# Paired transposes, deferred normalisation and early factors in a two-layer hybrid encoder kernel

## The chip, the cores and the metric

The kernel runs on one core of a Trainium2 chip. The metric is device time in microseconds (us) of one execution; where several executions are given, it is their median. The profile of the kernel before comes from one further execution, taken by the hardware profiler.

## The reference

Two layers (DEPTH = 2) work on x of 512 positions by 2048. In each layer:

```python
h = rmsnorm(x, pre_norm_g[l])
z = h @ w_in[l]                                   # 2048 -> 4928 columns
q_lat, kv_lat, k_pe, gb, gc, xin, q_mem, gate = split_cols(z)
q  = rmsnorm(q_lat, q_norm_g[l]) @ w_uq[l]        # 512 -> 8 heads of 192
kv = rmsnorm(kv_lat, kv_norm_g[l]) @ w_ukv[l]     # 256 -> 8 heads of 256
# rotary positions on the last 64 of each q head and on k_pe, shared by all heads
a_out = mla_attention(q, k, v)                    # softmax over all 512 positions
c_out = gb * conv3(gc * xin)
m_out = memory_attention(q_mem, rmsnorm(mem), w_mk[l], w_mv[l])   # 4 heads, 256 tokens
y = concat(a_out, c_out, m_out) * silu(gate)
x = x + rmsnorm(y @ w_o[l], post_norm_g[l])
```

Everything is float32. The kernel keeps that precision by splitting each operand of a product into a high and a low part and adding three products.

## The kernel before

**Products.** Every float32 operand is split: ScalarE casts it to the high part (`wh`, line 177; line 257 for activations), VectorE subtracts that from the source and leaves the low part (`wl`, line 178; line 258). `mm3` (lines 250 to 254) then issues three matmuls per pair of operands: high by high (252), high by low (253), low by high (254). Which of the two operands comes first decides whether line 253 or line 254 is the one that needs the low part of the weights. The large projections (input and output) multiply blocks by a scheme with seven products in place of eight; its passes are called P1 to P7, and each step of a pass (`step`, line 524) holds twelve matmuls of 512 columns: one unit of weights of 128 x 1024 against two blocks of rows. Sums of weights are made by accumulating DMAs that GpSimd issues (line 154).

**Layer.** A layer runs through five groups of columns of the input projection (`gs[0]` to `gs[4]`; group 3 makes the latents q_lat, kv_lat and k_pe, group 4 makes half of the gate), the turning of latents and gates, in layer 0 the memory's keys and values, then `mixer`: sixteen query blocks of memory attention (four heads of four blocks of 128 queries), thirty-two of the main attention (eight heads), and the output projection `out_proj`, whose last part adds the residual and, in layer 0, makes the normalised rows that layer 1 starts from. The memory's keys and values of layer 1 are woven between the first transposes of layer 1.

**Order.** The instructions of TensorE, SyncE and GpSimd run in the order in which the program issues them. The order on VectorE and ScalarE is chosen when the program is compiled, among what is ready by the compiler's own estimate, earlier issued work first. On the chip each engine keeps to its order.

**Planner.** `Program.run` (lines 118 to 205) goes through a list of steps. Ahead of each step it loads and prepares (casts and subtracts) the weights of the step itself and of the two units behind it. After the step it adds the step's `room` to a balance (at most 2.5), and takes put-off work from a queue as long as the balance covers the cost of the queue's head. `pr.defer(cost, fn)` puts work in that queue; `pr.until(cond)` issues from it until a condition holds. A step of the passes has a room of 1.4, less where its end brings work for VectorE.

**Latents.** `latents_begin` (line 820), put between the fourth and the fifth step of group 4, squares the eight latent blocks on ScalarE (line 808), makes the factors on GpSimd (`rsqrt_mean`, lines 262 and 264, and line 811), and issues eight products on VectorE at once (line 813). From the seventeenth step of group 4 on, `latent_turn` transposes the normalised latents.

**Attention.** `head_iters` makes three parts of each query block: `score` (matmuls of the scores, maximum on VectorE, line 995; exponential on ScalarE, 998; reciprocal on VectorE, 1000; scaling on ScalarE, 1001), `trans` (transposes of the 128 x 512 or 128 x 256 weights on TensorE, line 1012, into a PSUM bank, then the split into `PT`), and `av` (the product with the values, for two query blocks together). `pipeline` (line 1050) strings them: in iteration k comes the score of block k, then other work given in `between` (projections of the next heads, rotary steps, turned rotary queries), then `trans` of block k-3, and in each second iteration `av` of the blocks up to k-5. All tiles in PSUM share eight banks.

**Residual.** When a block of 128 rows of the output projection has its four column quarters (`scale`, line 1147), `residual` (line 1189) puts four or five pieces of work in the queue: `factor` (sum of squares and the factor on GpSimd, cost 0.2), two halves of the residual product (`part`, line 1205 on VectorE, cost 1.2 each, each followed by a store that GpSimd issues), and in layer 0 `norm`, which squares all 2048 columns on ScalarE (line 573), makes the next layer's factor on GpSimd and scales all columns (line 579).

Of the kernel before, what the change touches and what calls it, by code (L numbers as in the profile page):

```python
# [8 lines left out]
AF = mybir.ActivationFunctionType  # L9
ALU = mybir.AluOpType  # L10
# [3 lines left out]
D = 2048  # L14
S = 512
KT = D // P
NT = S // P
# [7 lines left out]
EPS = 1e-6  # L25
# [55 lines left out]
class Program:  # L81
# [19 lines left out]
    def add(self, fn, units=(), room=0.0, ahead=None):  # L101

        self.steps.append((list(units), fn, room, self.ahead if ahead is None else ahead))
# [104 lines left out]
def encoder(tc, x, mem, positions, pre_norm_g, w_in, q_norm_g, w_uq, kv_norm_g, w_ukv, conv_w,  # L208
# [3 lines left out]
    nc = tc.nc  # L212
# [15 lines left out]
    pr = Program(nc, raw_p, hi_p, lo_p)  # L228
    add = pr.add

    G = {}
    n_id = [0]

    def nm(s):
        n_id[0] += 1
        return f"{s}_{n_id[0]}"
# [4 lines left out]
    def slab(name, dt=F32):  # L241
        return slabs.tile([P, D], dt, tag="slab", name=nm(name))

    def scrap(name, w=512, dt=F32):
        return piece.tile([P, 512], dt, tag="piece", name=nm(name))[:, :w]

    def small(w=1, tag="st"):
        return stat.tile([P, w], F32, tag=tag, name=nm(tag))
# [7 lines left out]
    def split_to(hi, lo, src):  # L256
        nc.scalar.copy(hi, src)  # L257
        nc.vector.tensor_tensor(lo, src, hi.bitcast(F32), op=ALU.subtract)  # L258

    def rsqrt_mean(ssq, n, w=1, more=EPS):  # L260
        ms = small(w, "ms")
        nc.gpsimd.tensor_scalar(ms, ssq, 1.0 / n, more, op0=ALU.mult, op1=ALU.add)
        r = small(w, "r")
        nc.gpsimd.tensor_tensor(r, ms, G["mhalf"][:, :w], op=ALU.pow)
        return r
# [305 lines left out]
    def row_factor(xt, junk):  # L571
        ssq = small()
        nc.scalar.activation(junk, xt, AF.Square, accum_out=ssq)
        return rsqrt_mean(ssq, D)

    def normalise_rows(xt, dst, on=None):
        r = row_factor(xt, dst)
        if on is nc.scalar:
            nc.scalar.activation(dst, xt, AF.Copy, scale=r)
        else:  # L580
            nc.vector.tensor_scalar_mul(dst, xt, r)
# [182 lines left out]
    def turn4(view, j, dst=None):  # L764

        ps = bank("tps")
        for t in range(NT):
            nc.tensor.transpose(ps[:, t * P:(t + 1) * P], view(t)[:, j * P:(j + 1) * P], G["ident"])  # L768
        return ps
# [6 lines left out]
    def gate_turn(j, view, c):  # L776
        def f():
            ps = turn4(view, c)
            nc.scalar.activation(y_slab(j // 4)[:, j % 4, :], ps, AF.Silu)
        return f  # L780
# [13 lines left out]
    def qm_turn(j, C):  # L794
        def f():
            if j == 0:
                G["Qm"] = tuple(slab(n, F32R).rearrange("p (i c) -> p i c", i=4) for n in ("QmH", "QmL"))
            ps = turn4(lambda t: C["qm"][:, t, :], j)
            hi, lo = G["Qm"][0][:, j, :], G["Qm"][1][:, j, :]
            nc.scalar.activation(hi, ps, AF.Copy, scale=SC_MEM)  # L800
            nc.vector.scalar_tensor_tensor(lo, ps, SC_MEM, hi.bitcast(F32), op0=ALU.mult, op1=ALU.subtract)
        return f

    def normalise(views, n, gain, by=None):
        junk, grow = scrap("junk", n), gain
        ssq = small(NT, "ssq4")
        for t, v in enumerate(views):
            nc.scalar.activation(junk, v, AF.Square, accum_out=ssq[:, t:t + 1])
        r = rsqrt_mean(ssq, n, NT)
        if by:  # L810
            nc.gpsimd.tensor_scalar(r, r, by, None, op0=ALU.mult)
        for t, v in enumerate(views):
            nc.vector.scalar_tensor_tensor(v, v, r[:, t:t + 1], grow, op0=ALU.mult, op1=ALU.mult)

    def latents_rows(l):
        G["grow"] = scrap("growq"), scrap("growk", KVR)
# [3 lines left out]
    def latents_begin(l, C):  # L820
        G["q"] = [v[:, :QR_] for v in C["lat"]]
        G["kv"] = [v[:, O_KV:O_KV + KVR] for v in C["lat"]]
        normalise(G["q"], QR_, G["grow"][0], SC_MLA)
        normalise(G["kv"], KVR, G["grow"][1])

    def k_rope(C):
        m = scrap("kpm").rearrange("p (b t s i) -> p b t s i", b=2, t=NT, s=2)
        m1, m2 = m[:, 0], m[:, 1]
        for t in range(NT):
            kp = C["lat"][t][:, O_PE:O_PE + ROPE].rearrange("p (s i) -> p s i", s=2)  # L830
            nc.vector.tensor_tensor(m1[:, t], kp, G["cos2"][:, t], op=ALU.mult)
            for s in range(2):
                nc.vector.tensor_tensor(m2[:, t, s, :], kp[:, 1 - s, :], G["sin2"][:, t, s, :], op=ALU.mult)
        nc.vector.tensor_tensor(m1, m1, m2, op=ALU.add)
        kr = m1.rearrange("p t s i -> p t (s i)")
        krA = scrap("krA", dt=F32R).rearrange("p (t d i) -> p t d i", t=NT, d=2)
        krB = scrap("krB", dt=F32R).rearrange("p (t d i) -> p t d i", t=NT, d=2)
        for d in range(2):
            nc.scalar.copy(krA[:, :, d, :], kr)
            nc.vector.tensor_tensor(krB[:, :, d, :], kr, krA[:, :, d, :].bitcast(F32), op=ALU.subtract)  # L840
        G["kr"] = krA, krB
# [7 lines left out]
            nc.scalar.copy(kab[:, n * S:(n + 1) * S], ps.bitcast(F32))  # L849
        G["KA"], G["KB"] = kab[:, :S], kab[:, S:2 * S]  # L850

    def latent_turn(tag, j):
        def f():
            if j == 0:
                if tag == "cq":
                    G["cq"] = tuple(slab(n, F32R).rearrange("p (k c) -> p k c", c=S) for n in ("cqH", "cqL"))
                else:
                    both = slab("ckv", F32R).rearrange("p (s k c) -> p s k c", s=2, k=2)
                    G["ckv"] = both[:, 0], both[:, 1]
            views = G["q" if tag == "cq" else "kv"]  # L860
            ps = turn4(lambda t: views[t], j)
            H, L = G[tag]
            split_to(H[:, j, :], L[:, j, :], ps)
        return f
# [184 lines left out]

    def pipeline(its, between):  # L1050

        n = len(its)
        for k in range(max(n + 6, max(between) + 1)):
            if k < n:
                add(*its[k][0])
            for s in between.get(k, ()):
                add(*s)
            if 0 <= k - 3 < n:
                add(its[k - 3][1])
            if 0 <= k - 5 < n and its[k - 5][2]:  # L1060
                add(its[k - 5][2])

# [7 lines left out]
    def mixer(l, C, gates, pair2, tail):  # L1070
# [27 lines left out]
        for pair in range(4):  # L1098
# [5 lines left out]
            for k, v in nxt.items():  # L1104
                between[m + 8 * pair + k] = v
        pipeline(its, between)


# [80 lines left out]
    def residual(l, st, t):  # L1189
        last = l == depth - 1  # L1190
        rows = slice(t * P, (t + 1) * P)
        og = st["og"][t]

        def factor():
            if last and t == NT - 1:
                st["r", t] = rsqrt_mean(st["ssq"][t][:, 2:3], D, more=st["pre"])
                return
            tot = small(1, "tot2")
            nc.vector.tensor_reduce(tot, st["ssq"][t], axis=AX.X, op=ALU.add)
            st["r", t] = rsqrt_mean(tot, D)  # L1200

        def part(c, n=1024):
            cs = slice(c, c + n)
            xt = st["x"][t]
            nc.vector.scalar_tensor_tensor(xt[:, cs], og[:, cs], st["r", t], xt[:, cs], op0=ALU.mult, op1=ALU.add)
            if last:
                nc.sync.dma_start(out[0][rows, cs], xt[:, cs])
            else:
                nc.gpsimd.dma_start(G["dst"][rows, cs], xt[:, cs])

        def norm():
            normalise_rows(st["x"].pop(t), og, on=nc.scalar)
            G[f"hs{t}"] = og

        pr.defer(0.2, factor)
        pr.defer(1.2, lambda: part(0))
        if last and t == NT - 1:
            pr.defer(0.7, lambda: part(1536, 512))
            pr.defer(0.7, lambda: part(1024, 512))
        else:  # L1220
            pr.defer(1.2, lambda: part(1024))
        if not last:
            pr.defer(0.0, norm)
# [8 lines left out]
    def put(*passes):  # L1232
        for steps in passes:
            for s in steps:
                add(*s)
# [26 lines left out]
    for l in range(depth):  # L1262
# [22 lines left out]
        else:  # L1285
# [3 lines left out]
            for n in range(16):  # L1289
                t, q = n // 4, n % 4  # L1290
# [41 lines left out]
        if l == 0:  # L1332
            add(positions_load)
        g4 = [s for steps in gs[4] for s in steps]
        put(g4[:4])
        add(lambda l=l, C=C: latents_begin(l, C))
        put(g4[4:8])
        if l > 0:
            add(lambda C=C: k_rope(C))
        put(g4[8:16])  # L1340
        if l == 0:
            add(mem_load)
            G["mTd"] = dram.tile([4, P, D], F32, name="mTd")
        lat = [latent_turn("cq", j) for j in range(4)] + [latent_turn("ckv", j) for j in range(2)] + [k_rope_turn] * (l > 0)
        gm = lambda t, C=C: C["gm"][:, t, :]
        more = [(f, []) for f in lat + [qm_turn(j, C) for j in range(4)] + [gate_turn(12 + j, gm, j) for j in range(4)]]
        if l == 0:
# [74 lines left out]
```

## Time and profile before

| | us |
|---|---|
| median of 3 runs (1511.77 to 1512.84) | 1511.78 |
| the profiled execution | 1512.46 |
| its span | 1510.7 |
| TensorE busy | 1488.4 |
| VectorE busy | 1054.7 |
| ScalarE busy | 869.3 |
| GpSimd busy | 291.3 |

The span is the time from the first to the last instruction of the profiled execution. In the rows of the timeline below the columns are: start from the span's beginning in us, duration in us, engine (PE is TensorE, ACT ScalarE, DVE VectorE, POOL GpSimd), line of the kernel, operation, output and inputs, shape, number of instructions merged in the row, and in brackets the engine's idle time before it with what ended the wait. Matmuls overlap: the duration of one of 512 columns is given as 0.39, but the next one starts 0.23 later, so time lost is read from the starts.

### The profile page before, as it was taken

How to read it: one execution, taken by the hardware profiler on the slowest of the kernel's cores; microseconds unless marked ns; L12 is line 12 of the kernel's file. 1: busy time of each engine (PE TensorE's matmuls, PEld its weight loads, DVE VectorE, ACT ScalarE, POOL GpSimd, SP SyncE). 2: the span in 40 equal slices, each digit the busy share in tenths (PEclk: the TensorE clock that was granted, in tenths of full speed). 3: DMA queues.
4: the chain of work that ended last, by engine and by line, in shares of the span. 5: the costliest groups of instructions: out<-in, count | busy, mean ns of one | idle time of the engine just before them, and what ended most of it. 6: DMA issues, size and time to landing. Idle time of an engine off the chain costs nothing.

```text
span 1510.7 us, 20218 instructions
## 1 busy us (share of the span) xinstructions
PE 1488.4 (99%) x7613; PEld 1277.4 (85%) x7613; DVE 1054.7 (70%) x1404; ACT 869.3 (58%) x1347; POOL 291.3 (19%) x289
## 2 busy tenths in 40 slices
PE   9999999999999999999999999999999999999997
PEld 7888888988898888888888888888988888888886
DVE  6965675555868668769788765675565486698687
ACT  7743534454767768645588533534454587686443
POOL 1233131332000000230220233121333000003212
PEclk9999999999999999999999999999999999999999
DMA  8999897989582111595987999897989521027945
GB/s 332 217 212 224 202 177 167 199 202 248 167 262 80 52 41 58 103 212 159 306 293 246 238 219 224 198 171 167 204 196 212 159 71 43 29 84 138 259 118 182
DMA packets 142580, 267.18 MB, mean 177 GB/s; under 512 B 17084, under 2 KB 39956, under 8 KB 139156
## 3 DMA queue, kind: packets, MB, share of 16 engines
q0 software_dynamic: 59072, 128.99, 44.3%
q1 hardware_dynamic: 83280, 136.88, 27.9%
q8 instruction: 59, 0.97, 0.3%
q14 instruction: 37, 0.30, 0.1%
q10 hardware_dynamic: 132, 0.05, 0.0%
HBM read 251.20 MB, written 14.68 MB: 176 GB/s over the span
## 4 chain that ended last, share of the span: by engine, by line
PE 90%; ACT 3%; DVE 3%; issue 2%; POOL 1%; DMA 1%; POOLq 0%; DVEq 0%; ACTq 0%
PE P L253 21%; PE P L254 21%; PE P L252 21%; PE ptp L1012 2%; PE tps L768 2%; PE o L253 1%; PE o L254 1%; PE o L252 1%; PE mk L253 1%; PE sc L252 1%; POOL wr L137 1%; PE mk L254 1%; PE sc L253 1%; PE mk L252 1%; PE sc L254 1%
## 5 line engine op out<-in xcount | busy, mean ns | idle before, releaser
L178 DVE TENSOR_TENSOR wl<-wr,wh 128x1024 fp32r<-128x1024 f32 (+1 forms) x400 | 476.2, 1195 | 316.1 <-ACT wh L177 315.4
L177 ACT CAST wh<-wr 128x1024 fp32r<-128x1024 f32 (+1 forms) x400 | 411.6, 1032 | 465.6 <-PE P L254 398.2
L253 PE MATMUL P<-wl,S 128*128 128x512 f32 (+1 forms) x896 | 344.0, 384 | 2.8 <-DVE wl L178 2.8
L252 PE MATMUL P<-wh,S 128*128 128x512 f32 (+1 forms) x896 | 346.1, 386 | 0.2 <-ACT wh L177 0.2
L254 PE MATMUL P<-wh,S 128*128 128x512 f32 (+1 forms) x896 | 343.5, 383 | 0.0
L137 POOL DMA_DIRECT2D wr<-in_w_in_dram x160 | 193.5, 1210 | 484.0 <-DVE wl L178 351.8
L252 PE MATMUL P<-wh,A 128*128 128x512 f32 (+1 forms) x656 | 253.6, 387 | 0.8 <-ACT og L498 0.6
L253 PE MATMUL P<-wl,A 128*128 128x512 f32 (+1 forms) x656 | 251.9, 384 | 1.8 <-DVE wl L178 1.8
L254 PE MATMUL P<-wh,A 128*128 128x512 f32 (+1 forms) x656 | 251.8, 384 | 0.5 <-DVE A L258 0.5
L253 PEld LDWEIGHTS P<-wl,S 128*128 128x128 f32 x896 | 168.3, 188 | 33.0 <-DVE wl L178 4.0
L254 PEld LDWEIGHTS P<-wh,S 128*128 128x128 f32 x896 | 168.2, 188 | 30.7
L252 PEld LDWEIGHTS P<-wh,S 128*128 128x128 f32 x896 | 168.2, 188 | 30.1 <-ACT wh L177 0.6
L137 POOL DMA_DIRECT2D wr<-in_w_o_dram x40 | 48.4, 1209 | 531.9 <-DVE wl L178 516.6
L253 PEld LDWEIGHTS P<-wl,A 128*128 128x128 f32 x656 | 123.3, 188 | 23.6 <-DVE wl L178 2.5
L254 PEld LDWEIGHTS P<-wh,A 128*128 128x128 f32 x656 | 123.1, 188 | 23.5 <-DVE A L258 1.2
L252 PEld LDWEIGHTS P<-wh,A 128*128 128x128 f32 x656 | 123.1, 188 | 23.3 <-ACT og L498 1.0
L998 ACT ACTIVATE P<-sc,nm 128x512 f32<-128x512 f32 (+1 forms) x96 | 59.9, 624 | 32.4 <-DVE nm L995 32.0
L1001 ACT ACTIVATE P<-P,rec 128x512 f32<-128x512 f32 (+1 forms) x96 | 61.9, 658 | 4.6 <-DVE rec L1000 4.6
L995 DVE TENSOR_REDUCE nm<-sc 128x1 f32<-128x512 f32 (+1 forms) x96 | 57.1, 595 | 10.5 <-PE sc L993 6.9
L258 DVE TENSOR_TENSOR PT<-ptp,PT 128x512 fp32r<-128x512 f32 (+1 forms) x96 | 56.8, 593 | 7.7 <-ACT PT L257 7.3
L183 DVE SCALAR_TENSOR_TENSOR wl<-wr,cols,wh 128x512 fp32r<-128x512 f32 x64 | 46.2, 746 | 15.8 <-ACT wh L182 14.5
L182 ACT ACTIVATE wh<-wr,cols 128x512 fp32r<-128x512 f32 x64 | 44.4, 720 | 21.0 <-PE mk L253 9.0
(280 smaller groups left out, 2225.8 us busy)
## 6 DMA issues: line engine op xcount, KB each, us to landing
wr<-in_w_in_dram POOLq DMA_DIRECT2D x128, 512.0 KB, 6.9
wr<-in_w_in_dram SPq DMA_DIRECT2D x112, 512.0 KB, 5.6
wr<-in_w_o_dram SPq DMA_DIRECT2D x48, 512.0 KB, 4.0
wr<-in_w_o_dram POOLq DMA_DIRECT2D x40, 512.0 KB, 7.1
wr<-in_w_in_dram POOLq DMA_DIRECT2D x32, 416.0 KB, 5.7
wr<-in_w_in_dram SPq DMA_DIRECT2D x24, 416.0 KB, 4.2
wr<-in_w_mk_dram SPq DMA_DIRECT2D x16, 512.0 KB, 4.9
wr<-in_w_mv_dram SPq DMA_DIRECT2D x16, 512.0 KB, 5.0
```

The source lines that it names most:

```text
L137: engine.dma_start(dst, src, **kw)
L177: nc.scalar.copy(hi[:, :n], src)
L178: nc.vector.tensor_tensor(lo[:, :n], src, hi[:, :n].bitcast(F32), op=ALU.subtract)
L182: nc.scalar.activation(hi[:, h], src[:, h], AF.Copy, scale=g)
L183: nc.vector.scalar_tensor_tensor(lo[:, h], src[:, h], g, hi[:, h].bitcast(F32), op0=ALU.mult, op1=ALU.subtract)
L252: nc.tensor.matmul(ps, ah, bh, start=first, stop=False, **kw)
L253: nc.tensor.matmul(ps, ah, bl, start=False, stop=False, **kw)
L254: nc.tensor.matmul(ps, al, bh, start=False, stop=last, **kw)
L258: nc.vector.tensor_tensor(lo, src, hi.bitcast(F32), op=ALU.subtract)
L995: nc.vector.tensor_reduce(nmax, ps, axis=AX.X, op=ALU.max, negate=True)
L998: nc.scalar.activation(pt, ps, AF.Exp, bias=nmax, accum_out=tot)
L1001: nc.scalar.activation(pt, pt, AF.Copy, scale=rec)
```

## The change

Four edits:

1. `normalise` issues its eight products of the latents no longer at once, but puts each in the queue with a cost of 0.7, and a mark `normalised` behind them. `latents_begin` moves up by two steps, to stand between the second and the third step of group 4. The first `latent_turn` of each kind issues what is still queued up to the mark.
2. In `pipeline`, odd iterations transpose blocks k-3 and k-2, even iterations none.
3. `residual` makes its factor as soon as it is called, and no longer through the queue. In the last layer's last block the factor uses the same sums as before.
4. In layer 0 each `part` is followed by the square of its half on ScalarE. `norm` no longer squares all columns: it adds the first half's share and the epsilon on GpSimd, makes the factor from that and the second half, and scales the two halves in two instructions.

```diff
     def normalise(views, n, gain, by=None):
...
-        for t, v in enumerate(views):
-            nc.vector.scalar_tensor_tensor(v, v, r[:, t:t + 1], grow, op0=ALU.mult, op1=ALU.mult)
+        def times(t, v):
+            return lambda: nc.vector.scalar_tensor_tensor(v, v, r[:, t:t + 1], gain, op0=ALU.mult, op1=ALU.mult)
+        for t, v in enumerate(views):
+            pr.defer(0.7, times(t, v))
...
         normalise(G["kv"], KVR, G["grow"][1])
+        pr.defer(0.0, lambda: G.update(normalised=l))
...
             if j == 0:
+                pr.until(lambda: G.get("normalised") == l)
...
     def pipeline(its, between):
...
-            if 0 <= k - 3 < n:
-                add(its[k - 3][1])
+            for b in (k - 3, k - 2) if k % 2 else ():
+                if 0 <= b < n:
+                    add(its[b][1])
...
     def residual(l, st, t):
...
-        def factor():
-            if last and t == NT - 1:
-                st["r", t] = rsqrt_mean(st["ssq"][t][:, 2:3], D, more=st["pre"])
-                return
+        if last and t == NT - 1:
+            st["r", t] = rsqrt_mean(st["ssq"][t][:, 2:3], D, more=st["pre"])
+        else:
             tot = small(1, "tot2")
             nc.vector.tensor_reduce(tot, st["ssq"][t], axis=AX.X, op=ALU.add)
             st["r", t] = rsqrt_mean(tot, D)
...
                 nc.gpsimd.dma_start(G["dst"][rows, cs], xt[:, cs])
+                col = c // 1024
+                nc.scalar.activation(og[:, cs], xt[:, cs], AF.Square, accum_out=squares[:, col:col + 1])
+
+        squares = None if last else small(NT, "ssq4")
 
         def norm():
-            normalise_rows(st["x"].pop(t), og, on=nc.scalar)
+            xt = st["x"].pop(t)
+            half = small(1, "tot2")
+            nc.gpsimd.tensor_scalar(half, squares[:, :1], 1.0 / D, EPS, op0=ALU.mult, op1=ALU.add)
+            r = rsqrt_mean(squares[:, 1:2], D, more=half)
+            for c in range(2):
+                nc.scalar.activation(og[:, c * 1024:(c + 1) * 1024], xt[:, c * 1024:(c + 1) * 1024], AF.Copy, scale=r)
             G[f"hs{t}"] = og
 
-        pr.defer(0.2, factor)
...
-        put(g4[:4])
+        put(g4[:2])
         add(lambda l=l, C=C: latents_begin(l, C))
-        put(g4[4:8])
+        put(g4[2:8])
```

More of the change, by code (lines that the diff above doesn't have):

```diff
@@ L804, in normalise @@
     def normalise(views, n, gain, by=None):
-        junk, grow = scrap("junk", n), gain
+        junk = scrap("junk", n)
         ssq = small(NT, "ssq4")
@@ L850, in k_rope_turn, with latent_turn @@
         G["KA"], G["KB"] = kab[:, :S], kab[:, S:2 * S]
-    def latent_turn(tag, j):
+    def latent_turn(l, tag, j):
         def f():
             if j == 0:
+                pr.until(lambda: G.get("normalised") == l)
                 if tag == "cq":
@@ L1343, in encoder @@
             G["mTd"] = dram.tile([4, P, D], F32, name="mTd")
-        lat = [latent_turn("cq", j) for j in range(4)] + [latent_turn("ckv", j) for j in range(2)] + [k_rope_turn] * (l > 0)
+        lat = [latent_turn(l, "cq", j) for j in range(4)] + [latent_turn(l, "ckv", j) for j in range(2)] + [k_rope_turn] * (l > 0)
         gm = lambda t, C=C: C["gm"][:, t, :]
```

## The prediction

> **What bounds the kernel now.** I read the page's first lines first, then the waits of TensorE, then the timelines of the places where it waits, and the busy time by stretch.
>
> ```profile
> span 1510.7 us, 20218 instructions
> PE 1488.4 (99%) x7613; PEld 1277.4 (85%) x7613; DVE 1054.7 (70%) x1404; ACT 869.3 (58%) x1347; POOL 291.3 (19%) x289
> ```
>
> TensorE is idle for 1510.7 - 1488.4 = 22.3 us of the span. No edit removes a matmul or a transpose, so nothing beyond that idle time, and what a wait costs around itself, can be gained; and most of it lies at the start and the end of the run, where the edits change nothing. What counts is whether a wait of TensorE goes away or a new one comes. The first kind of place is in group 4, once per layer:
>
> ```profile
> 333.51 0.39 PE L252 MATMUL P<-wh,S 128*128 128x512 f32 x1
> 334.94 0.50 PE L253 MATMUL P<-wl,S 128*128 128x512 f32 x1 [1.04 <-DVE wl L178]
> 335.28 0.40 PE L254 MATMUL P<-wh,S 128*128 128x512 f32 x1
> 335.51 0.39 PE L252 MATMUL P<-wh,S 128*128 128x512 f32 x1
> 1127.22 0.50 PE L253 MATMUL P<-wl,S 128*128 128x512 f32 x1 [1.04 <-DVE wl L178]
> ```
>
> Undisturbed, a matmul of 512 columns starts 0.23 after the one before (335.28 to 335.51). Here it came 334.94 - 333.51 - 0.23 = 1.20 late, and the one after it took 0.11 more than 0.23. So a wait shown as 1.04 costs 1.31: the idle time shown plus 0.27. Layer 1 has the same 1.04.
>
> The second place is memory attention:
>
> ```profile
> 470.00:492.00 22.00, 20.22 (x142) 17.43 (x140) 19.92 (x55) 20.64 (x60) 0.00 (x0) 1.00 0.23 69
> 492.00:605.00 113.00, 113.00 (x670) 98.97 (x669) 82.26 (x142) 84.36 (x167) 0.00 (x0) 1.00 0.15 48
> ```
>
> The columns are the stretch, its length, the busy time of TensorE, of its weight loads, of VectorE, ScalarE and GpSimd, and the granted clock. From 470 to 492 TensorE idles for 1.78 us while ScalarE is busy for 20.64 of 22 and VectorE for 19.92: both are full, and TensorE goes at their pace. In the main attention (492 to 605) TensorE never idles and the others have a quarter of their time free.
>
> **The latents' products.** The late operand above is a subtraction that stood behind the eight products on VectorE:
>
> ```profile
> 329.40 2.77 DVE L813 SCALAR_TENSOR_TENSOR lat<-lat,r,growq 128x512 f32<-128x512 f32 x4 [1.54 <-POOL r L811]
> 332.09 1.66 DVE L813 SCALAR_TENSOR_TENSOR lat<-lat,r,growk 128x256 f32<-128x256 f32 x4
> 333.67 3.48 DVE L178 TENSOR_TENSOR wl<-wr,wh 128x1024 fp32r<-128x1024 f32 x3
> 328.75 1.05 ACT L177 CAST wh<-wr 128x1024 fp32r<-128x1024 f32 x1
> 322.83 1.20 POOL L137 DMA_DIRECT2D wr<-in_w_in_dram  x1 [1.08 <-DVE wl L178]
> 325.55 1.20 POOL L137 DMA_DIRECT2D wr<-in_w_in_dram  x1 [1.52 <-DVE wl L178]
> 329.13 0.23 POOL L811 TENSOR_SCALAR r<-r 128x4 f32<-128x4 f32 x1
> 329.72 1.35 POOL L264 TENSOR_TENSOR r<-ms,mhalf 128x4 f32<-128x4 f32 x1
> ```
>
> Its cast was done at 328.75 + 1.05 = 329.80; it ran at 333.67, after 2.77 + 1.66 = 4.4 us of products. A subtraction takes 3.48 / 3 = 1.2, and TensorE wanted the result at 333.74.
>
> The edit moves the factors two steps up. On GpSimd they then stand behind the DMA of 322.83 and ahead of the one of 325.55, that is 2.7 us earlier: q's factor at about 329.36 - 2.7 = 326.6, the other at 331.07 - 2.7 = 328.4. The DMA passed over goes out at about 328.4 in place of 325.55; its unit is the first of the next pass, eight units on, and the products of those take 8 x 12 x 0.23 = 22 us, which covers it. The next such DMA waits for the very subtraction that was late and goes out earlier.
>
> The products are now emitted as the balance allows: 2.5 at first (three products), then 1.4 per step, so 3, 2, 2 and 1. Between two subtractions stand at most three products, 3 x 2.77 / 4 = 2.1 us, in place of 4.4, and they begin 2.7 us earlier. The subtraction of 333.67 can then run at about 330.4. Both waits go: 2 x 1.31 = 2.6. Bounds: if the compiled order puts the four q products and one more ahead of the subtraction next in turn (ready at 326.6, wanted at 331.0), it ends near 327.3 + 2.77 + 0.42 + 1.23 = 331.7 and is 0.7 late: gain 0.6 per layer, 1.2. No gain at all is a rival below. I take 2.5. The squares on ScalarE ran as their latents came; that they are issued earlier I cost at nothing. `until` finds the mark set, ten steps ahead.
>
> **Pairs of transposes.** What a change between products and transposes costs:
>
> ```profile
> 613.09 0.39 PE L993 MATMUL sc<-KAB,QR 128*128 128x512 f32 x1
> 613.32 0.60 PE L1012 MATMUL ptp<-identr,P 128*128 128x128 f32 x4
> 613.68 0.48 PE L252 MATMUL P<-wh,A 128*128 128x512 f32 x1
> 613.99 0.39 PE L253 MATMUL P<-wl,A 128*128 128x512 f32 x1
> 1192.51 1.91 PE L768 MATMUL tps<-identr,gm 128*128 128x128 f32 x16
> 1194.26 1.91 PE L768 MATMUL tps<-identr,ga 128*128 128x128 f32 x16
> 1195.92 0.47 PE L252 MATMUL qr<-wh,cqH 128*128 128x512 f32 x1
> 1196.23 0.39 PE L253 MATMUL qr<-wl,cqH 128*128 128x512 f32 x1
> ```
>
> Four transposes between products take 613.99 - 613.32 - 0.23 = 0.44; in a run, (1194.26 - 1192.51) / 4 = 0.44 too. A change costs 0.00 to 0.01, and 48 of 96 blocks lose theirs: 0 to 0.5, I take 0.3.
>
> So this edit lives by waits. An odd block is transposed one iteration earlier, while its score stays where it is:
>
> ```profile
> 484.85 0.39 PE L253 MATMUL o<-PT,Vm 128*128 128x256 f32 x1 [0.32 <-DVE PT L258]
> 487.97 0.51 ACT L1001 ACTIVATE P<-P,rec 128x256 f32<-128x256 f32 x1
> 488.99 0.44 PE L1012 MATMUL ptp<-identr,P 128*128 128x128 f32 x2 [0.34 <-ACT P L998]
> 610.75 0.38 PE L253 MATMUL o<-PT,V 128*128 128x256 f32 x1 [0.17 <-DVE PT L258]
> 613.38 0.71 ACT L1001 ACTIVATE P<-P,rec 128x512 f32<-128x512 f32 x1
> ```
>
> The values' product gains a whole iteration of lead: its waits for `PT` (0.32 at 484.85, 0.17 at 610.75) should go, worth 0.6 and 0.4 with the 0.27. The transposes lose one. In memory attention the block of 488.99 already waits for its weights (0.34; its scaling ends at 487.97 + 0.51 = 488.48). It would now come up before 488, ahead of a score and eight turned queries that used to fill that time; behind it these queue up. ScalarE and VectorE, which are full there, have the same work, so TensorE should leave the stage when they do: bounds from all of the 1.78 (and as much again around the waits) gained to the same lost; I take 0.2 lost per layer. In the last pair of heads one odd block would stand at 613.32 + 0.44 = 613.76, against weights that end at 613.38 + 0.71 = 614.09; the 0.4 saved upstream is spent there. Net 0.1 gained per layer, bounds 0.4 either way. Elsewhere the main attention has no wait, and two banks of PSUM held at once instead of one fall on engines with a quarter of their time free; if that cover went, a block would cost its 0.27 and more. Sum for the edit: 0.3 - 0.4 + 0.2 = 0.1 gained.
>
> **Factors and halves.** These matter between the layers:
>
> ```profile
> 748.58 1.92 ACT L573 ACTIVATE og<-xr 128x2048 f32<-128x2048 f32 x1
> 751.55 2.01 ACT L579 ACTIVATE og<-xr,r 128x2048 f32<-128x2048 f32 x1 [0.49 <-POOL r L264]
> 753.47 1.99 ACT L177 CAST wh<-wr 128x1024 fp32r<-128x1024 f32 x2
> 751.88 0.55 POOL L264 TENSOR_TENSOR r<-ms,mhalf 128x1 f32<-128x1 f32 x1
> 752.46 1.29 DVE L1205 SCALAR_TENSOR_TENSOR xr<-og,r,xr 128x1024 f32<-128x1024 f32 x1 [2.23 <-POOL r L264]
> 754.27 1.28 DVE L1205 SCALAR_TENSOR_TENSOR xr<-og,r,xr 128x1024 f32<-128x1024 f32 x1
> 755.46 1.22 DVE L178 TENSOR_TENSOR wl<-wr,wh 128x1024 fp32r<-128x1024 f32 x1
> 751.11 0.50 PE L252 MATMUL P<-wh,A 128*128 128x512 f32 x1 [0.55 <-ACT og L498]
> 756.73 0.50 PE L253 MATMUL P<-wl,A 128*128 128x512 f32 x1 [1.02 <-DVE wl L178]
> ```
>
> TensorE loses 0.55 + 0.27 = 0.8 to a copy out of PSUM that stood behind the 1.92 square, and 1.02 + 0.27 = 1.3 to a subtraction: its cast stood behind the 2.01 scaling until 753.47, and it stood itself behind the second block's product of 754.27. That block's factor came from GpSimd at 751.88, queued behind the first block's normalisation, and VectorE waited 2.23 for it. With factors at once it is there before 746, and the second block's products can use that idle 2.23. With halves, the first half is squared while VectorE makes the second product, so the copy comes about a half square (1.0) earlier: 0.6 of the 0.8 gained. The scaling ends 0.4 earlier, the subtraction need not wait for 754.27: together 0.5 of the 1.3. I take 1.0 gained. At best both waits go, 2.1. At worst the second block's squares, which can now start earlier, run ahead of the cast: 1.9 more there, less the 0.8 gained: 1.1 lost.
>
> The halves add per block one square, one scaling (a 2048 row split in two costs about 0.1 more each), one reading of the sum and one operation on GpSimd, some 0.5 in all, four times; after 757 it lies beside TensorE's work on the memory's keys and values, and if that cover went, 2 us. Behind a factor that waits on GpSimd stand only the residual's own stores, needed a layer later. In the last layer the last block's factor waits for the same sums as before: nothing.
>
> **Sum.** 2.5 + 0.1 + 1.0 = 3.6 off the span: 1507.1. The profiled execution took 1512.46, that is 1.76 outside its span, and stood 0.68 above the median 1511.78; against the median, 1508.2.
>
> **Rivals.** *The odd block's wait takes over (slower).* In memory attention the second transposes of a pair stand at the head of TensorE's queue until ScalarE has scaled their weights; scores behind them wait, so ScalarE gets its next scores later and the lag stays. Price: eight odd blocks per layer, each with the 0.34 that one shows already, plus 0.27: 16 x 0.61 = 9.8 lost, against the 2.5 + 0.3 + 0.2 + 1.0 = 4.0 of the other terms: 1517.6. It decides from 4.0 / 16 = 0.25 per odd block on; at 0.4 per block the time is 1514.2. For it: ScalarE and VectorE are full; against: their work is not more. *The products still stand ahead.* VectorE's compiled order keeps them in one run: latents gain nothing, 1510.7. For it: VectorE ran them in one run although the program could be ordered otherwise; against: they are now issued behind later subtractions. *The boundary loses.* The second block's squares come ahead of the cast: 1.1 lost where 1.0 was gained, 1510.3. *More goes.* Memory attention's waits vanish too, with 1.78 idle per layer: 3.6 plus 0.2 x 2 more, 1504.2. *The clock.*
>
> ```profile
> 1.61 6.59 PE L1229 MATMUL warm<-identr 128*128 128x128 f32 x37 [1.61 <-DVE identr L275]
> ```
>
> At the start 37 transposes took 6.59, 0.18 each, against 0.11 in the run of 1192.51. Were transposes in pairs to run at the early pace, 320 x 0.07 = 22 us: 1530. Against it: two runs of sixteen, one behind the other, kept 0.11, and the products behind them are spaced as behind four (0.31 from 1195.92 to 1196.23, as from 613.68 to 613.99); the clock granted in the stage itself is 1.00. The Trainium skill, "TensorE: Matmul & The Clock Gate", Part 4: PE-mode transpose, says that transposes do not count as busy time for TensorE's clock gate, which speaks against longer runs of them. By that rule the time would be the 1530 of this rival; for runs as short as these the trace does not agree, at 0.11 per transpose.
>
> **How the numbers follow.** Forecast 0.50 (its own range 1506.5 to 1510), odd blocks 0.14, products 0.12, boundary 0.12, more 0.11, clock 0.01. About 0.2%, 3.0 us, is what a measurement of this kernel can tell from no change. Faster, below 1508.8: 0.36 of the forecast, all of "more", 0.02 of the boundary, 0.49. Same: 0.14 of the forecast, products, the rest of the boundary, and 0.04 of the odd blocks, 0.40. Slower, above 1514.8: 0.10 of the odd blocks, and the clock, 0.11. The range leaves out the far halves of "more" and "odd blocks": 1504.5 to 1513.
>
> **What would show it.** Right: no wait of line 253 behind line 178 in group 4, products of line 813 with subtractions between them; line 1012 in rows of 8 and 4; no wait of `o` for `PT`; the second block's line 1205 without the 2.23; TensorE idle some 3 us less. Wrong: waits of line 1012 or of scores for ScalarE of more than 3.5 us a layer from 470 to 492, a wait of line 252 for `wh` near 755, or any wait in the main attention.

## The result, and the profile after

The changed kernel took 1522.28 us (median of four runs, 1519.17 to 1524.32) against 1511.78 before: a ratio of 1.0068, 95% interval 1.0049 to 1.0087. It is slower, by some 10 us; the forecast was 1508.2 with a range up to 1513, so size and sign were both wrong. The profiled execution took 1522.7 and stands close to the median.

First the head of the page after; the columns are as before.

```profile
span 1520.7 us, 20238 instructions
PE 1491.7 (98%) x7613; PEld 1282.3 (84%) x7613; DVE 1055.5 (69%) x1404; ACT 871.5 (57%) x1359; POOL 295.7 (19%) x293
```

The span grew by 10.0. TensorE's idle time went from 22.3 to 1520.7 - 1491.7 = 29.0, that is 6.7 of them; the other 3.3 are *busy* time, with the same 7613 instructions: some ran slower. The waits of TensorE over the whole run (waiter, waited for, us in total, times, longest) say where the idle time is:

```profile
PE ptp L1017 <- ACT P L1006: 6.6, 4, 2.0
PE P L252 <- ACT og L498: 5.2, 1, 5.2
PE P L253 <- DVE wl L178: 1.8, 3, 0.8
```

The third row had been 4.6 us in five waits: the latents' edit worked. The first two are new in size: transposes waiting for scaled weights (twice per layer), and one wait of 5.2 for a copy out of PSUM between the layers.

To find all of the 10.0, I summed per stage how much later than its nominal spacing each TensorE instruction started (0.23 for a product of 512 columns, 0.11 for a transpose, as in the prediction). Idle time, what a wait costs around itself and slow stretches all count in it. Worked out from TensorE's timelines of before and after, in us:

| stage | before | after | difference |
|---|---|---|---|
| latents, layers 0 and 1 | 1.30 + 1.29 | 0.59 + 0.09 | -1.9 |
| memory's keys and values, layer 1 (775 to 830) | 0.27 | 0.82 | +0.5 |
| memory attention, layers 0 and 1 | 3.07 + 3.10 | 3.26 + 3.26 | +0.3 |
| last pair of heads, layers 0 and 1 | 0.77 + 0.78 | 2.50 + 4.06 | +5.0 |
| between the layers | 2.14 | 8.17 | +6.0 |

They add to 10.0, as much as the span grew. The start of the run took 0.5 longer as well (28 of its 60 transposes ran 0.21 apart and not 0.11, before 23), and small gains elsewhere give most of that back. The 0.5 of the second row is in no other run, and no experiment explains it. Two places carry the loss.

**Between the layers.** The timelines of VectorE, GpSimd, ScalarE and TensorE after, from 744 to 757 (start, duration, engine, line, operation):

```profile
744.27 1.29 DVE L1211 SCALAR_TENSOR_TENSOR xr<-og,r,xr 128x1024 f32<-128x1024 f32 x1 [0.66 <-POOL r L264]
...
751.27 1.28 DVE L1211 SCALAR_TENSOR_TENSOR xr<-og,r,xr 128x1024 f32<-128x1024 f32 x1
...
749.25 3.35 POOL L262 TENSOR_SCALAR ms<-ssq,tot 128x1 f32<-128x1 f32 x1 [0.18 <-POOL tot L1224]
752.68 0.56 POOL L264 TENSOR_TENSOR r<-ms,mhalf 128x1 f32<-128x1 f32 x1
...
753.27 2.19 ACT L1227 ACTIVATE og<-xr,r 128x1024 f32<-128x1024 f32 x2 [1.87 <-POOL r L264]
755.37 1.05 ACT L498 COPY og<-P 128x512 f32<-128x512 f32 x2
...
750.42 0.39 PE L254 MATMUL P<-wh,S 128*128 128x512 f32 x1
755.98 0.80 PE L252 MATMUL P<-wh,A 128*128 128x512 f32 x1 [5.18 <-ACT og L498]
756.57 0.63 PE L253 MATMUL P<-wl,A 128*128 128x512 f32 x1
757.00 0.63 PE L254 MATMUL P<-wh,A 128*128 128x512 f32 x1
```

Read it from the end. TensorE stands from 750.8 to 755.98 because its next product needs a PSUM bank that line 498 copies out; the first of the two copies ends about 755.9. The copies are ready to go long before, but in ScalarE's compiled order they stand behind the scaling of line 1227, and that waits for a factor from GpSimd. GpSimd is late because one operation on 128x1 values took 3.35 us; before, the same line took 0.19. It ends at 752.60, and VectorE, at work without a pause since 744.27, pauses from 752.55 (751.27 + 1.28). So the factor came as early as I forecast, the second block's products did use the idle 2.23; but that pause was what let GpSimd run.

Behind the wait the clock falls. The windows of memory attention and right behind the two places (stretch, length, busy time of TensorE, weight loads, VectorE, ScalarE, GpSimd, granted clock, DMA share, GB/s):

```profile
470.00:492.00 22.00, 19.60 (x140) 17.34 (x141) 19.94 (x56) 20.79 (x62) 0.00 (x0) 1.00 0.20 62
...
615.40:619.00 3.60, 3.58 (x19) 3.07 (x20) 1.55 (x5) 2.47 (x6) 0.00 (x0) 1.00 0.00 0
756.00:762.00 6.00, 6.00 (x15) 4.70 (x16) 3.17 (x4) 3.51 (x7) 0.83 (x2) 0.51 1.01 375
1366.00:1369.60 3.60, 3.60 (x12) 2.96 (x11) 1.29 (x3) 2.09 (x5) 0.00 (x0) 0.53 0.02 5
```

From 756 to 762 the clock is 0.51, and products start 0.43 apart instead of 0.23 (756.57 to 757.00): fifteen of them, about 0.20 late each, are 3.0. With the 5.18 of the wait that is the 8.2 lost at this place, and most of the extra busy time.

**The last pair of heads.** ScalarE and TensorE in layer 0, after:

```profile
610.75 1.07 ACT L257 CAST PT<-ptp 128x512 fp32r<-128x512 f32 x2 [1.58 <-DVE S L258]
611.88 1.06 ACT L257 CAST S<-y 128x1024 fp32r<-128x1024 f32 x1
612.84 0.68 ACT L1003 ACTIVATE P<-sc,nm 128x512 f32<-128x512 f32 x1
613.51 0.57 ACT L257 CAST PT<-ptp 128x512 fp32r<-128x512 f32 x1
613.98 0.70 ACT L1003 ACTIVATE P<-sc,nm 128x512 f32<-128x512 f32 x1
614.65 0.72 ACT L1006 ACTIVATE P<-P,rec 128x512 f32<-128x512 f32 x1
612.61 0.39 PE L998 MATMUL sc<-KAB,QR 128*128 128x512 f32 x1
612.84 0.60 PE L1017 MATMUL ptp<-identr,P 128*128 128x128 f32 x4
615.42 0.66 PE L1017 MATMUL ptp<-identr,P 128*128 128x128 f32 x4 [1.98 <-ACT P L1006]
615.84 0.47 PE L252 MATMUL P<-wh,A 128*128 128x512 f32 x1
```

Block 45, the last odd one, is due at about 613.4 but its weights are ready at 614.65 + 0.72 = 615.37. ScalarE's work in this stretch belongs to two things at once: a pair of PT casts in place of one, and the casts of `S` that the next stage needs. In the kernel before, ScalarE made block 45's exponential first and the cast of `S` behind it:

```profile
611.33 0.69 ACT L998 ACTIVATE P<-sc,nm 128x512 f32<-128x512 f32 x1
612.42 1.05 ACT L257 CAST S<-y 128x1024 fp32r<-128x1024 f32 x1 [0.30 <-PE o L254]
```

Here the two PT casts and the cast of `S` (611.88) stand ahead of that exponential (612.84). VectorE adds to it: two subtractions for `PT` and one of `S` stand ahead of the block's maximum, which starts at 611.18, before at 610.62. The wait is 1.98 in each layer. In layer 0 the clock stays at 1.00 behind it, in layer 1 it falls to 0.53 (the windows above), which costs 1.6 more there.

In memory attention the profile shows two waits of 1.3 (of the 6.6 in four), yet the stage lost 0.17 per layer in net: from 470 to 492 ScalarE is busy for 20.79 us, as it was for 20.64, and TensorE leaves with it, at a clock of 1.00.

### The profile page after: what moved, and what is told of

It reads as the page before. It is cut to its first block, busy times and chain, and to the rows that moved or that the text cites. A ratio compares the mean times of both kernels' runs of the same rounds, so it can differ in the third digit from the quotient of the medians.

```text
span 1520.7 us, 20238 instructions
## 1 busy us (share of the span) xinstructions
PE 1491.7 (98%) x7613; PEld 1282.3 (84%) x7613; DVE 1055.5 (69%) x1404; ACT 871.5 (57%) x1359; POOL 295.7 (19%) x293
## 4 chain that ended last, share of the span: by engine, by line
PE 91%; ACT 3%; DVE 2%; issue 2%; POOL 1%; DMA 1%; POOLq 0%; DVEq 0%; ACTq 0%
PE P L253 21%; PE P L252 21%; PE P L254 21%; PE ptp L1017 2%; PE tps L768 2%; PE o L254 1%; PE o L252 1%; PE o L253 1%; PE sc L252 1%; PE sc L253 1%; PE sc L254 1%; PE mk L254 1%; PE mk L253 1%; PE mk L252 1%; PE mv L252 1%
```

## The experiments

The kernel before ran beside each on the same chip; its median there stands in brackets, and the ratios and their intervals are against it (a ratio can differ a little from that of the two medians). Losses in a stage are worked out as in the table. Line numbers differ a little between kernels.

### Each edit alone

**latents_alone**: edit 1 only.

> Only the first edit: the latents' products put off, their factors two steps earlier. Theory (the trace of the changed kernel read place by place): this edit is the one that does what it says; it takes back 0.7 in layer 0 and 1.2 in layer 1, so 1509.9. Rival (it only trades waits): some wait of TensorE for VectorE or GpSimd comes up elsewhere and the time stays within 1 us of 1511.8.

Measured: 1510.87 [1513.79], ratio 0.9985 (0.9974 to 0.9995). In group 4 TensorE has no wait left in either layer; the stage loses 0.11 and 0.10 in place of 1.30 and 1.29. The mechanism and its size hold: 2.4 in the stage, 0.15% in the time.

**pairs_alone**: edit 2 only.

> Only the second edit: two blocks' weights transposed together. Theory: odd blocks reach TensorE before ScalarE has scaled their weights. In the last pair of heads that costs 1.7 per layer (a wait of some 2.0 at the second of two transposes), in memory attention 0.2 per layer, and where the wait of 2.0 lets the granted clock fall, another 1.6: 1515 to 1517.5. Rival (the boundary between the layers, not the pairs, spoils the clock and the last pair): the pairs by themselves are within 1 us of 1511.8.

Measured: 1517.92 [1513.79], ratio 1.0024 (1.0013 to 1.0035). TensorE's waits from 600 to 660, and the window behind the same place of layer 1:

```profile
PE ptp L1012 <- ACT P L1001: 2.0, 1, 2.0
...
1360.00:1364.00 4.00, 3.85 (x13) 3.11 (x14) 1.67 (x5) 2.47 (x6) 0.00 (x0) 0.60 0.01 4
```

The wait of 2.0 and the fall of the clock in layer 1 come from this edit alone: the last pairs lose 2.49 and 4.05, as in the whole change.

**factors_alone**: edit 3 only.

> Only the third edit: the residual's factors at once, the normalisation still over all columns. Theory: the second block's products then follow on VectorE without a pause, GpSimd's small operations for the normalisation take over 1 us in place of 0.2 as long as VectorE does not pause, ScalarE's scaling comes later and the cast behind it too: TensorE loses 2 to 4 us more between the layers, 1514 to 1516. Rival (the halves alone are at fault): the factors at once save 0.5 to 1.3, 1510.5 to 1511.3.

Measured: 1517.43 [1513.79], ratio 1.0021 (1.0008 to 1.0033). GpSimd, ScalarE and TensorE's wait between the layers:

```profile
747.63 0.20 POOL L262 TENSOR_SCALAR ms<-st 128x1 f32<-128x1 f32 x1 [1.30 <-ACT og L573]
747.91 3.22 POOL L264 TENSOR_TENSOR r<-ms,mhalf 128x1 f32<-128x1 f32 x1
...
751.17 2.00 ACT L579 ACTIVATE og<-xr,r 128x2048 f32<-128x2048 f32 x1 [2.21 <-POOL r L264]
753.08 0.56 ACT L498 COPY og<-P 128x512 f32<-128x512 f32 x1
...
PE P L252 <- ACT og L498: 3.7, 2, 3.0
```

The same chain without the halves. Here it is the next GpSimd operation that is held (3.22 where before had 0.55); it ends at 751.13, 0.41 behind VectorE's row (750.03 + 0.69). The stage loses 7.04 instead of 2.14, and the clock from 750 to 757 is 0.71.

**halves_alone**: edit 4 only.

> Only the fourth edit: squares by halves behind each product, scaling in halves, factors still through the queue. Theory: VectorE still pauses for the second block's factor, GpSimd's small operations keep their 0.2 to 0.6, and the boundary gets no worse: 1510.5 to 1512. Rival (the order on ScalarE alone is at fault, with the copy out of PSUM behind the scaling): a wait of several us for line 498, 1514 to 1518.

Measured: 1513.08 [1513.79], ratio 0.9997 (0.9987 to 1.0006): no difference that can be told. In the trace the stage loses 1.37 in place of 2.14, and GpSimd's operations take 0.2 to 1.1. The halves by themselves do no harm; with the factors left in the queue, VectorE still pauses.

The four ratios add up to +0.27%, the whole has +0.68%. At the boundary the trace shows 4.9 lost by the factors and 0.8 gained by the halves, and 6.0 lost by both: 1.9 more than the sum. The slow stretch behind the wait is some 6 us in both (clock 0.50 from 753.7 to 759.7 in factors_alone). What differs is TensorE's waits, 5.2 against 3.7: with both edits *both* copies stand behind the scaling, while factors_alone still has one ahead of it (748.38); and the halves' 0.8 does not come. The rest of the difference isn't settled; each of the single ratios is uncertain by 0.1%.

### What holds the boundary up

**vector_filled**: the kernel before, with three VectorE additions put into its pause. They add up a half of the residual into a scratch tile that nothing reads.

```diff
                 nc.gpsimd.dma_start(G["dst"][rows, cs], xt[:, cs])
+                if t == 0 and c:
+                    more = raw_p.tile([P, 1024], F32, tag="raw", name=nm("fill"))
+                    for _ in range(3):
+                        nc.vector.tensor_tensor(more, xt[:, cs], xt[:, cs], op=ALU.add)
```

> The kernel before, with three additions of 128x1024 on VectorE added behind the first block's second residual product (their result is used nowhere), so that VectorE does not pause there while GpSimd makes the factor. Theory (GpSimd's small operations stand still as long as VectorE runs without a pause): one of GpSimd's operations of the first block's normalisation takes 1.5 to 3.5 us in place of 0.2 to 0.6, and TensorE loses 2 to 4 us more between the layers. Rival (what held GpSimd was its own queue, the loads and stores issued there): its operations keep 0.2 to 0.6, and TensorE loses at most 1 us, by VectorE's extra 3.6 us of work.

Measured: 1517.80 [1512.92], ratio 1.0029 (1.0019 to 1.0039). GpSimd, the last filling addition, and TensorE's waits between the layers:

```profile
751.56 3.61 POOL L262 TENSOR_SCALAR ms<-st 128x1 f32<-128x1 f32 x1 [1.28 <-ACT og L573]
...
753.91 1.22 DVE L1213 TENSOR_TENSOR fill<-xr 128x1024 f32<-128x1024 f32 x1
...
PE P L252 <- ACT wh L177: 2.5, 1, 2.5
PE P L253 <- DVE wl L178: 0.8, 1, 0.8
PE P L252 <- ACT og L498: 0.6, 1, 0.6
```

None of the four edits is in this kernel. The GpSimd operation that took 0.19 takes 3.61 and ends at 755.17; VectorE is without a pause until 753.91 + 1.22 = 755.13. So a full VectorE is enough to hold the tiny operation. ScalarE's scaling and the cast behind it come late (the 2.5), the clock falls behind that (0.59 from 760 to 764), and the stage loses 6.12. The 0.8 may also be the additions' own time on VectorE.

**norm_later**: all four edits, but the normalisation enters the queue with a cost of 1.4 instead of 0.0, so that in ScalarE's order the copies of line 498 stand ahead of the scaling.

```diff
-            pr.defer(0.0, norm)
+            pr.defer(1.4, norm)
```

> The changed kernel with all four edits, but the normalisation of the next layer costs 1.4 in the queue in place of 0.0, so that it is issued a step later and ScalarE's order has both copies out of PSUM (line 498) and one more cast ahead of the scaling. Theory (the long wait of 5.2 is ScalarE's scaling, held by GpSimd's factor, standing ahead of a copy that TensorE needs): the wait of line 498 falls below 1 us, the granted clock stays at 1.00 between the layers, and some 6 us come back: 1515 to 1517. GpSimd's operation for the factor may still take over 1 us. Rival (GpSimd's late factor holds TensorE by whatever way): line 498 is replaced by another wait of similar length, 1520 to 1523.

Measured: 1515.47 [1512.92], ratio 1.0012 (1.0002 to 1.0022), from 1.0068. GpSimd, VectorE, ScalarE, TensorE's wait and the window:

```profile
747.82 5.69 POOL L262 TENSOR_SCALAR ms<-ssq,tot 128x1 f32<-128x1 f32 x1 [0.18 <-POOL tot L1224]
...
752.24 1.22 DVE L178 TENSOR_TENSOR wl<-wr,wh 128x1024 fp32r<-128x1024 f32 x1
...
749.88 1.05 ACT L498 COPY og<-P 128x512 f32<-128x512 f32 x2
754.18 2.19 ACT L1227 ACTIVATE og<-xr,r 128x1024 f32<-128x1024 f32 x2 [2.30 <-POOL r L264]
...
PE P L252 <- ACT og L498: 1.1, 1, 1.1
...
750.00:755.00 5.00, 4.50 (x20) 3.70 (x21) 3.46 (x4) 2.70 (x4) 4.90 (x4) 1.00 1.00 362
```

GpSimd is held even longer, 5.69, until 753.51; VectorE runs until 752.24 + 1.22 = 753.46. But now nothing that TensorE needs stands behind the scaling: the wait is 1.1 (below 1 was expected), the clock 1.00, the stage loses 1.42 in place of 8.17. So the loss needs two things: the held operation, and work that TensorE needs behind the instruction that waits for it, here a copy out of PSUM, in vector_filled a cast. What is left over the kernel before sits in the last pairs of heads: 2.46 and 2.49 lost. In the profiled execution, the quickest of ten (1512.86), the clock stayed up there and its mean over the run was 0.999; in eight of the other nine it was 0.996 or 0.997. That the last pair's wait lowers it in those is likely from pairs_alone, but no trace of them shows the place.

### What the last pair of heads waits for

**pairs_but_one**: edit 2 alone, but block 45 keeps its old iteration.

```diff
-            if 0 <= k - 3 < n:
-                add(its[k - 3][1])
+            for b in (k - 3, k - 2) if k % 2 else ():
+                if 0 <= b < n and b != n - 3:
+                    add(its[b][1])
+            if k == n:
+                add(its[n - 3][1])
```

> The second edit alone, but block 45 (the second of the next to last pair, in the last pair of heads) is transposed in its old place, one iteration later. Theory (one block per layer costs the 1.7, and the clock's fall behind it 1.6 in layer 1): back to within 1 us of the kernel before; the last pair of heads loses 0.4 to 1.0 per layer, memory attention keeps its 0.2. Rival (any odd block there would wait, or the wait moves to block 47 or to the values' product): 2 to 4 us above the kernel before.

Measured: 1511.53 [1512.92], ratio 0.9989 (0.9979 to 0.9999). From 604 to 630 TensorE has no wait, and the last pairs lose 0.30 and 0.29, less than the 0.77 of before. Of 24 odd blocks per layer, one carried the loss.

**pairs_late**: the pairs are made of blocks k-4 and k-3 on even iterations, so no block is turned early and half of them one iteration late.

```diff
-            if 0 <= k - 3 < n:
-                add(its[k - 3][1])
+            for b in (k - 4, k - 3) if k % 2 == 0 else ():
+                if 0 <= b < n:
+                    add(its[b][1])
```

> The kernel before, with pairs formed the other way round: even iterations transpose blocks k-4 and k-3, so that the odd block keeps its place and the even one comes an iteration later. Theory (the loss of the pairs comes from the odd block's place, an iteration early, not from two transposes in a row): the wait of 2.0 in the last pair of heads is gone in both layers, each loses 0.2 to 1.0 there, and the time is within 1.5 of the kernel before. Rival (two transposes in a row, with two banks held and two splits queued on ScalarE and VectorE, are the cost): 1.5 to 3 lost per layer again, 3 us or more above the kernel before.

Measured: 1512.77 [1513.96], ratio 0.9992 (0.9982 to 1.0001). Waits from 600 to 630:

```profile
PE o L253 <- DVE PT L258: 0.4, 1, 0.4
PE o L252 <- ACT P L998: 0.3, 1, 0.3
```

Also two in a row, and yet the wait of 2.0 is gone: the early place is the cost, not the pair. It isn't free, though: the values' products now wait for `PT`, and the last pairs lose 1.69 and 1.70, more than the 0.2 to 1.0 that was expected.

**sums_later**: edit 2 alone, with the first sums of the output projection, whose casts and subtractions of `S` run beside block 45, at iteration 48 instead of 40.

```diff
-        last_pair = {0: [(sums(0), []), g0[0][0]], ...
-                     4: [g1[0][0]], 8: [g1[0][1]], ...
+        last_pair = {0: [g0[0][0]], ...
+                     4: [g1[0][0]], 8: [(sums(0), []), g1[0][1]], ...
```

> The second edit alone, with the first half's sums and splits for the output projection (casts of 1.05 on ScalarE and subtractions of 1.22 on VectorE) issued in iteration 48, behind block 45, in place of iteration 40. Theory (block 45's weights are late because these long casts and subtractions stand between its score and its scaling): the wait at block 45 falls from 2.0 to less than 0.7 per layer, though the sums may then be late for the output projection. Rival (the casts of the blocks transposed just before, 42 and 43, stand ahead of block 45's exponential on ScalarE and are enough by themselves): the wait stays above 1.3.

Measured: 1522.90 [1513.96], ratio 1.0055 (1.0038 to 1.0072). Waits from 604 to 660, and the window of the output projection's start:

```profile
PE P L252 <- ACT A L257: 2.3, 1, 2.3
PE P L254 <- DVE A L258: 1.4, 1, 1.4
...
615.00:660.00 45.00, 41.38 (x192) 34.03 (x191) 40.52 (x42) 29.06 (x38) 13.98 (x13) 0.92 0.70 120
```

Block 45's wait is gone, and the last pairs lose 0.13 and 0.12: the work on `S` was what kept its weights. But the output projection now waits for its operands: TensorE idles for 3.6 of 45 us there and the clock falls to 0.92. That confirms the reason; as a repair it is useless.

### A kernel without the two losses

**three_mended**: edits 1 and 4, edit 2 with block 45 at its old iteration, and the factors through the queue as before.

> First, second and fourth edit, factors through the queue as before, block 45 in its old place. Theory: latents 2.4 gained, halves 0.8, pairs between 0.3 gained and 0.3 lost: 1508.0 to 1509.5 where the kernel before has 1511.8, ratio 0.9975 to 0.9990. Rival (the edits hide each other's waits): within 1 us of the kernel before.

Measured: 1509.34 [1512.92], ratio 0.9974 (0.9965 to 0.9982), 3.6 us quicker than the kernel before, and by its ratio well under the 1.0068 of the changed one. By stage: latents 0.69 and 0.12, last pairs 0.31 and 0.28, boundary 1.36; against before that is 1.8, 1.0 and 0.8 gained. That the total equals the 3.6 forecast for all four edits is a coincidence: the terms differ, and this is another kernel.

## Why the prediction was wrong

**The latents' products: right in kind, a little too large.** 1.9 of the forecast 2.5 in the whole change. In layer 0 it went as the lower bound said. VectorE and TensorE after:

```profile
327.63 2.76 DVE L814 SCALAR_TENSOR_TENSOR lat<-lat,r,growq 128x512 f32<-128x512 f32 x4 [1.53 <-POOL r L811]
330.32 0.47 DVE L814 SCALAR_TENSOR_TENSOR lat<-lat,r,growk 128x256 f32<-128x256 f32 x1
330.71 1.21 DVE L178 TENSOR_TENSOR wl<-wr,wh 128x1024 fp32r<-128x1024 f32 x1
...
331.98 0.50 PE L253 MATMUL P<-wl,A 128*128 128x512 f32 x1 [0.33 <-DVE wl L178]
```

Four q products and one more ran ahead of the subtraction, and 0.33 of wait with what lies around it is left: I had priced that case at 0.7 late, for both layers. The rival that the products stay in one run is out.

**Pairs: the sum of 0.1 gained failed at the last pair of heads.** The transitions and the values' waits for `PT` went about as said (the main attention lost 0.1 less per layer), and memory attention lost 0.17 per layer against a forecast 0.2. There the odd blocks' wait did appear, 1.3 in one block, but TensorE left the stage when the full engines did, as argued; the rival that charged 0.61 for each of sixteen odd blocks had the right sign and the wrong place. The step that failed is "one odd block would stand at 613.76, against weights that end at 614.09". I had moved TensorE's side of that comparison and left ScalarE's where it was. On ScalarE a pair of transposes brings a pair of casts, and the scores reach it in another rhythm; beside the casts of `S`, and VectorE's subtractions of it, the weights came at 615.37. The term was 0.1 gained per layer, with bounds of 0.4; it was 1.7 lost in layer 0 and 3.3 in layer 1.

**The boundary: the step "the second block's products can use that idle 2.23" was carried out, and was the mistake.** I took GpSimd's 0.55, 0.23 and the like as durations of the operations. They were durations beside a VectorE that paused. The trace of before already held a warning that I didn't read: on GpSimd,

```profile
742.31 1.51 POOL L264 TENSOR_TENSOR r<-ms,mhalf 128x1 f32<-128x1 f32 x1
750.68 0.19 POOL L262 TENSOR_SCALAR ms<-st 128x1 f32<-128x1 f32 x1 [1.28 <-ACT og L573]
```

The first took 1.51 beside a subtraction on VectorE, where the prediction's row of 751.88 has 0.55 for the same operation in VectorE's pause. My lower bound (1.1 lost) went by the second block's squares running ahead of a cast; the price came from another row of ScalarE's order, the scaling ahead of two copies out of PSUM. I had followed the copy only as far as "comes about a half square earlier" and not asked what stands ahead of it if the scaling's factor is late. Forecast 1.0 gained, bounds 2.1 gained to 1.1 lost; measured 6.0 lost.

**The clock** had a chance of 0.01 through transposes in rows, and that way it did not come: behind the pairs the clock is 1.00 in the window of memory attention above. The 0.18 per transpose on which that rival rests was a mean of two paces: in the same trace the first 23 of 60 transposes in a row start 0.21 apart and the others, from 6.5 us on, 0.11, while TensorE ran nothing else. So a row of transposes alone came to the full pace. (The profile's granted clock reads 1.00 in both stretches; the starts show the change.) It fell behind waits, which I had priced at 0.27 above their length; that surcharge is too small for the two longest. The rows named as signs did their work in part: the only wait "in the main attention" was the one of block 45; waits from 470 to 492 stayed below 3.5.

## What to carry to other kernels

An engine's pause can be what another engine lives on: before filling it, look at who runs in it, and price that one's work by the row where the filled engine was busy. When an operand may come late, look in the compiled order of the engine that waits for it at every instruction behind the waiting one, and above all for a copy that frees a PSUM bank; keep these ahead (one changed cost took 1.0068 back to 1.0012). And where an instruction is moved to an earlier place, work out again when its operand is ready at the *end* of a stage, where the next stage's preparation already runs on the engines that make it.

## What the hardware showed that was not expected

A GpSimd operation on 128x1 values lasted 3.35, 3.22, 3.61 and 5.69 us where 0.19 to 0.56 is usual; in after, vector_filled and norm_later it ended within 0.05 us after VectorE's last instruction of an unbroken row, most of them products and subtractions with two operands in SBUF. The Trainium skill, "SBUF — State Buffer", section "Who interferes with whom", says that a VectorE instruction with two SBUF inputs contends with a GpSimd instruction that reads SBUF, and that the later one is blocked until the first is through. The traces agree, and go further: in these cases GpSimd did not get in between consecutive VectorE instructions of 1.2 us each, but waited for several of them. It is not always so: earlier in the same row of after, two such operations (744.32 and 745.69) took 1.29 and 1.41 and got through while VectorE's row went on, and the 3.22 of factors_alone ended 0.41 behind it. What decides how long one is held, no run here shows.

TensorE's clock fell to about half after a wait of 5.18 (0.51 for 6 us), and after one of 1.98 in layer 1 (0.53 for 3.6 us), while the same 1.98 in layer 0 left it at 1.00. It fell too behind a wait of 3.03 in factors_alone (0.50 for 6 us) and behind waits of 2.47 and 0.76 close together in vector_filled (0.59 for 4 us). The Trainium skill, "TensorE: Matmul & The Clock Gate", Part 1, What's actually happening, puts the fall down to an idle window of about 3.4 us that runs freely. The 5.18 agrees, and a window that runs freely would explain why the same wait does different things in two layers; that 1.98 can be enough, or 3.03, does not follow from it. Around it lie transposes: from the last product's start to the next product's, TensorE did only those for 3.2 us (612.61 to 615.84 in layer 0). Whether they count as idle there, no run here separated; at the start of the run a row of nothing but transposes went from 0.21 to 0.11 apart.
